# Attention scores with the high-times-low product as two 64-row matmuls, and the value halves added on GpSimd

## The chip, the cores and the metric

One NeuronCore of a Trainium2 chip runs one program. Its engines have queues of their own and meet only at semaphores: TensorE (PE in the profile, with its weight loads as PEld), VectorE (DVE), ScalarE (ACT), GpSimd (POOL) and SyncE (SP), which issues most of the transfers. The metric is the device time of the program in microseconds (us), taken as the median of several runs. One further execution is recorded by the hardware profiler, and every duration below comes from that one.

## The reference, cut to what matters

The program is a two-layer encoder on a sequence of 1024 positions with 1024 channels: layer one mixes by attention, layer two by a long convolution, and each is followed by a gated feed-forward block. The change lies in the attention, which has 16 query heads of 64 channels that share 4 key and value heads in groups of 4:

```python
q = q.reshape(Bsz, L, N_HEADS, HEAD_DIM)
k = k.reshape(Bsz, L, N_KV_HEADS, HEAD_DIM)
...
q = apply_rope(rmsnorm(q, q_gain), cos, sin)
k = apply_rope(rmsnorm(k, k_gain), cos, sin)
...
def block(q_blk):
    s = jnp.einsum('bqkgd,bskd->bkgqs', q_blk, k, preferred_element_type=jnp.float32) * scale
    p = jax.nn.softmax(s, axis=-1).astype(v.dtype)
    return jnp.einsum('bkgqs,bskd->bqkgd', p, v)
```

Everything is float32, and the output has to keep close to that. The matmuls run in a float32 format that is rounded on the way in, so the kernel splits an operand into a rounded high part and the low part that is left, and adds up products of the parts.

## The kernel before, in words

The attention is worked off in 32 blocks: 4 key heads (`g`) times 8 tiles of 128 queries (`qb`). A block `u` holds the 4 query heads that share the key head, so it has 4 scores of 128 queries by 1024 keys, and 8 steps over tiles of 128 keys (`sb`).

- **Layout of the queries and keys.** `q_t` (`load_q`, line 811) has the 64 channels of the high part in partitions 0 to 63 and those of the low part in 64 to 127. `kTh` has the high keys in both halves of the partitions, `kTl` the low keys in both halves. So a matmul of all 128 rows of `q_t` with `kTh` (line 830) is high times high plus low times high, and one with `kTl` (line 831) is high times low plus low times low. A score takes four matmuls of 512 columns: two halves of the keys, each with both products, into two banks of PSUM.
- **Softmax.** VectorE takes the row maximum from PSUM (`nmx`, line 838), ScalarE the exponential with its row sum (`p_t`, line 848).
- **The steps.** For each tile of keys TensorE transposes the four heads' probabilities into one PSUM bank (`pt_ps`, line 854), ScalarE copies the high part out (`pT_hi`, line 859), VectorE subtracts it from PSUM for the low part (`pT_lo`, recorded under the helper's line 162), and two steps later TensorE multiplies both with the values (lines 872 and 873). The values `vst` hold the high part in 64 columns and the low part in the other 64, so the accumulator `o_ps` has two halves of 64 partitions that must still be added.
- **The end of a block** (`finish`). ScalarE copies each half out of `o_ps` by two copies of 64 by 256 that put the heads in place (`o_s`, `o_l`, line 893). VectorE adds the halves (line 895). TensorE transposes the reciprocal sums, spread out on GpSimd (`rbs`, line 885), into a bank of the same three that `pt_ps` uses (`rb_ps`, line 899). VectorE multiplies (line 900), which frees that bank, and GpSimd writes the high and low part of the result (lines 902 and 903).
- **What else runs there.** GpSimd works off 24 steps of a modulation vector between the blocks (`mod_step`, lines 189 to 192: one or two passes over 128 by 1024), and issues the loads of `q_t` (line 815).

`o_ps` has one bank, `pt_ps` and `rb_ps` three, a score two at a time. The order on each engine in this stage is set by the framework's scheduler, which lays the instructions out by a simulated timeline when the program is built; after that each engine works strictly through its list. The functions that the change touches, with the lines that the profile names:

Of the kernel before, what the change touches and what calls it, by code (L numbers as in the profile page):

```python
# [7 lines left out]
F32 = mybir.dt.float32  # L8
F32R = mybir.dt.float32r
# [5 lines left out]
P = 128  # L15
# [6 lines left out]
HD = 64  # L22
# [93 lines left out]
def tile_kernel(ctx: ExitStack, tc: tile.TileContext, t: dict):  # L116
    nc = tc.nc
    mm = nc.tensor.matmul
    V = nc.vector
    ADD, SUB, MUL = ALU.add, ALU.subtract, ALU.mult  # L120
# [26 lines left out]
    qd = [tc.dram_tile([8, P, L], F32, name=f"qd{i}") for i in range(2)]  # L147
# [13 lines left out]
    def sub_lo(lo, src, hi):  # L161
        V.tensor_tensor(lo, src, hi.bitcast(F32), op=SUB)  # L162
# [140 lines left out]
    HS = (slice(0, 512), slice(512, L))  # L303
# [321 lines left out]
    with tc.tile_pool(name="x0", bufs=1) as xp:  # L625
# [7 lines left out]
        def load_ada(k):  # L633
            at = ada_tile()
            for i in (1, 0):
                nc.sync.dma_start(at[:, i], t["ada_t"][i, k])
            return at
# [33 lines left out]
        for k in range(KT):  # L671
            at = load_ada(k) if k >= ADA0 else ada0[k]
# [21 lines left out]
    kTh = [kv_pool.tile([P, L], F32R, name=f"kTh{g}") for g in range(NKV)]  # L694
    kTl = [kv_pool.tile([P, L], F32R, name=f"kTl{g}") for g in range(NKV)]
    v_pool = tc.alloc_tile_pool(name="vst", bufs=1)
    vst = [v_pool.tile([P, NKV, 2, HD], F32R, name=f"vst{j}") for j in range(NT)]
    q_pool = tc.alloc_tile_pool(name="q", bufs=4)
    at0 = tc.alloc_tile_pool(name="att0", bufs=4)
    with tc.tile_pool(name="qkv", bufs=1) as qp:  # L700
        def qtile(tag, bufs):
# [63 lines left out]
        for ch in (2, 0, 1):  # L765
# [7 lines left out]
            for j in range(NT):  # L773
                if j not in pqs:
                    pqs[j] = mt("qkv_mm", {2: "AAAABBAA", 0: "AABBAAAA", 1: "AAAABBBB"}[ch][j])
                    tj = slice(j * P, (j + 1) * P)
                    for k in range(KT):
                        wh, wl = w[k // 2]
                        cs = slice(512 * (k % 2), 512 * (k % 2) + 512)
# [26 lines left out]
    at = tc.alloc_tile_pool(name="att", bufs=1)  # L806
    s_psp = tc.alloc_tile_pool(name="att_s", bufs=1, space=PSUM)
    ps = tc.alloc_tile_pool(name="att_ps", bufs=1, space=PSUM, side="right")
    qg = {}

    def load_q(u):
        if u < NU:
            g, qb = divmod(u, NT)
            qg[u] = q_pool.tile([P, 4, P], F32R, name="q_t", tag="q_t")
            nc.gpsimd.dma_start(qg[u], qd[g // 2][4 * (g % 2):4 * (g % 2) + 4, :, qb * P:(qb + 1) * P]
                              .rearrange("h p q -> p h q"))

    NU = NKV * NT
    sums, pts, s_t, pt_t, o_t = {}, {}, {}, {}, {}

    def scores(u, i):
        if u >= NU:
            return
        g, qb = divmod(u, NT)
        if i == 0:
            load_q(u + 3)
        s_ps = s_psp.tile([P, L], F32, name="s_ps", tag="s", bufs=2)
        for hf in range(2):
            cs = slice(512 * hf, 512 * hf + 512)
            mm(s_ps[:, cs], lhsT=qg[u][:, i], rhs=kTh[g][:, cs], start=True, stop=False)  # L830
            mm(s_ps[:, cs], lhsT=qg[u][:, i], rhs=kTl[g][:, cs], start=False, stop=True)  # L831
        s_t[u, i] = s_ps

    def rowmax(u, i):
# [20 lines left out]
        pt_t[u, sb] = [tp]  # L855

    def pt_hi(u, sb):
        ph = at.tile([P, 512], F32R, name="pT_hi", tag="pT_hi", bufs=6)
        nc.scalar.copy(ph, pt_t[u, sb][0])  # L859
        pt_t[u, sb].append(ph)  # L860

    def pt_lo(u, sb):
        pl = at.tile([P, 512], F32R, name="pT_lo", tag="pT_lo", bufs=6)
        sub_lo(pl, pt_t[u, sb][0], pt_t[u, sb][1])
        pt_t[u, sb].append(pl)

# [8 lines left out]
    fin = {}  # L875

    def finish(u, step):
        if u < 0:
            return
        g, qb = divmod(u, NT)  # L880
        if step == 0:
            rinv = at.tile([P, 4], F32, name="rinv", tag="rinv", bufs=2)
            V.reciprocal(rinv, sums[u])
            rbs = at.tile([P, 4, HD], F32, name="rbs", tag="rbs", bufs=3)
            nc.gpsimd.tensor_copy(rbs, rinv.unsqueeze(2).to_broadcast([P, 4, HD]))
            fin["rbs", u] = rbs.rearrange("p (a b) d -> p a (b d)", b=2)
        elif step == 2:
            fin["ol"] = at.tile([P, 2, P], F32, name="o_l", tag="o_l", bufs=2)
            fin["os"] = at.tile([P, 2, P], F32, name="o_s", tag="o_s", bufs=2)
            for lo, nm in ((0, "os"), (HD, "ol")):  # L890
                ov = o_t[u][lo:lo + HD, :].rearrange("p (a b q) -> p b a q", b=2, q=P)
                for par in range(2):
                    nc.scalar.copy(fin[nm][par * HD:(par + 1) * HD], ov[:, par])
        elif step == 3:
            V.tensor_tensor(fin["os"], fin["os"], fin["ol"], op=ADD)
            rb = ps.tile([P, 512], F32, name="rb_ps", tag="pt", bufs=3)
            fin["rb"] = rb[:, 0:256].rearrange("p (a q) -> p a q", q=P)
            for hp in range(2):
                nc.tensor.transpose(fin["rb"][:, hp], fin["rbs", u][:, hp], ident)
            V.tensor_tensor(fin["os"], fin["os"], fin["rb"], op=MUL)  # L900
            dst = [o_[:, 2 * g:2 * g + 2, qb * P:(qb + 1) * P] for o_ in (oht, olt)]
            nc.gpsimd.tensor_copy(dst[0], fin["os"])
            nc.gpsimd.tensor_tensor(dst[1], fin["os"], dst[0].bitcast(F32), op=SUB)

    LAG, MOD0, MODD = 2, 27, 9
    for u in range(3):
        load_q(u)
    for i in range(4):
        scores(0, i)
        rowmax(0, i)  # L910
        softexp(0, i)
    steps = [(u, sb) for u in range(NU) for sb in range(NT)]
    for n in range(len(steps) + LAG):
        if n < len(steps):
            if steps[n][1] == 0:
                finish(steps[n][0], 0)
            transp(*steps[n])
            pt_hi(*steps[n])
            pt_lo(*steps[n])
        if n >= LAG:  # L920
            u, sb = steps[n - LAG]
            attend(u, sb)
            if sb == NT - 1:
                finish(u, 2)
                finish(u, 3)
        if n == 246:
            w_o0 = load_split(t["w_o"][0], w0_pool, 1)
        i, k = divmod((n - MOD0) // MODD, KT)
        if (n - MOD0) % MODD == 0 and 0 <= i < 3:
            mod_step(3 + i, ssq, k)  # L930
        if (n - MOD0) % MODD == MODD - 3 and k == KT - 1 and -1 <= i < 3:
            mod_fin(0, 3 + i, ssq, lambda: ps.tile([P, 512], F32, name="pt_ps", tag="pt", bufs=3))
        if n < len(steps):
            u, sb = steps[n]
            if sb < 4 and u + 1 < NU:
                scores(u + 1, sb)
                rowmax(u + 1, sb)
                softexp(u + 1, sb)
# [813 lines left out]
    with tc.manual_schedule(engines={mybir.EngineType.PE}):  # L1752
        w = sum(max(c - MM_CBASE, MM_CMIN) for n in range(G_END) for c in step_cost(n))
        rate = (1 + 21 * 48 + 2 * FLUSH - n_mm[0]) / w
        for n, c in conv_steps(JOBS, on_done):
            if gemm:
                owed += rate * max(c - MM_CBASE, MM_CMIN)
                need = {(1 + o, c4) for o, c4 in JOBS[:(n + 2) // 8]}
                while gemm and (owed >= 1 or n >= G_END or (n == 5 and len(ca) == 2) or need - seen):
                    g = next(gemm, None)  # L1760
# [275 lines left out]
```

## Time and profile before

| What | Value |
| --- | --- |
| Median of 3 runs (lowest, highest) | 2944.6 us (2941.42, 2945.13) |
| Profiled execution, its own time | 2945.4 us |
| Its span in the trace | 2943.4 us |
| Busy: PE / DVE / ACT / POOL | 2819.3 / 2330.6 / 1232.5 / 317.5 us |
| Attention stage in the trace | about 230 to 632 us |
| In that stretch: PE / DVE / ACT / POOL busy | 382.98 / 343.31 / 320.63 / 184.47 us |

A matmul's record runs from its start to the end of its result's way out, so neighbours overlap, and the distance between two starts says what one of them costs. "128*128" in a row is rows times columns of the array that the weights use; "128x512" is the output. "idle before" with an arrow names what ended an engine's wait.

### The profile page before, as it was taken

The numbers are of one execution on the slowest core, as the hardware profiler recorded it, in microseconds if no ns is written. First come the engines' busy times: TensorE is split into PE (matmuls) and PEld (weight loads), VectorE is DVE, ScalarE is ACT, GpSimd is POOL, SyncE is SP. The second block draws the span as 40 slices with busy tenths as digits, with TensorE's granted clock in tenths as the row PEclk, the third lists the DMA queues.
The fourth block names the chain that finished last, engine by engine and source line by source line (L and its number), as shares of the span: only waits on it lengthen the run. The fifth ranks groups of instructions, "written<-read, shape, count | busy, mean of one in ns | idle before, by whom it ended". The sixth has DMA issues, their size and how long they took to land.

```text
span 2943.4 us, 36504 instructions
## 1 busy us (share of the span) xinstructions
PE 2819.3 (96%) x13152; PEld 2301.5 (78%) x13152; DVE 2330.6 (79%) x3225; ACT 1232.5 (42%) x1996; POOL 317.5 (11%) x344
## 2 busy tenths in 40 slices
PE   5989999999999999999999999999989999999998
PEld 4777877778888887888777887887868788887887
DVE  8797989869988887877777885888978887777544
ACT  3547888843444444343332332323334433333211
POOL 0063564400000000111000000000000000000000
PEclk9999999999999999999999999999999999999999
DMA  7262222146444444755456665556664332224321
GB/s 277 91 184 63 58 74 55 52 150 210 139 164 160 164 164 172 223 174 152 159 182 194 216 211 185 184 166 200 224 208 154 122 101 86 85 79 143 122 86 58
DMA packets 220823, 433.72 MB, mean 147 GB/s; under 512 B 22146, under 2 KB 117154, under 8 KB 216164
## 3 DMA queue, kind: packets, MB, share of 16 engines
q1 hardware_dynamic: 185444, 389.44, 39.5%
q0 software_dynamic: 35200, 41.95, 5.3%
q8 instruction: 104, 1.70, 0.2%
q14 instruction: 75, 0.61, 0.1%
HBM read 304.42 MB, written 126.89 MB: 147 GB/s over the span
## 4 chain that ended last, share of the span: by engine, by line
PE 64%; DVE 9%; DMA 4%; issue 1%; ACT 1%; SPq 0%; DVEq 0%; ACTq 0%; POOLq 0%
PE w_ps L1063 26%; PE d_ps L183 14%; PE u_ps L1437 4%; PE d_ps L1296 2%; PE wo_y L183 2%; PE ab_ps L1573 2%; PE f_ps L183 2%; PE g_ps L358 2%; PE v_ps L358 1%; DVE prod L1643 1%; PE f_ps L578 1%; PE wout_y L1859 1%; PE f_ps L579 1%; PE wo_y L1036 1%; DMA rd<-fw 1%
## 5 line engine op out<-in xcount | busy, mean ns | idle before, releaser
L1155 ACT CAST w_hi<-u 128x1024 fp32r<-128x1024 f32 x120 | 125.8, 1049 | 236.0 <-PE w_ps L1063 224.7
L162 DVE TENSOR_TENSOR pT_lo<-pt_ps,pT_hi 128x512 fp32r<-128x512 f32 x256 | 167.7, 681 | 46.9 <-ACT pT_hi L859 45.2
L1063 PE MATMUL w_ps<-t_h,w_hi 128*128 128x512 f32 x480 | 190.7, 397 | 1.9 <-ACT w_hi L1155 1.9
L1261 DVE SCALAR_TENSOR_TENSOR xd<-d_ps,mod,xd 128x1024 f32<-128x1024 f32 x104 | 132.7, 1280 | 75.4 <-PE d_ps L183 75.2
L1063 PE MATMUL w_ps<-t_h,w_lo 128*128 128x512 f32 x480 | 189.9, 397 | 0.7 <-DVE w_lo L162 0.7
L162 DVE TENSOR_TENSOR w_lo<-u,w_hi 128x1024 fp32r<-128x1024 f32 x120 | 146.6, 1222 | 55.6 <-ACT w_hi L1155 55.4
L1063 PE MATMUL w_ps<-t_l,w_hi 128*128 128x512 f32 x480 | 190.2, 396 | 0.0
L859 ACT CAST pT_hi<-pt_ps 128x512 fp32r<-128x512 f32 x256 | 145.0, 588 | 69.6 <-PE pt_ps L854 63.9
L183 PE MATMUL d_ps<-s_hi,wd_lo 128*128 128x512 f32 x544 | 170.0, 391 | 0.0
L183 PE MATMUL d_ps<-s_lo,wd_hi 128*128 128x512 f32 x544 | 169.9, 391 | 0.0
L183 PE MATMUL d_ps<-s_hi,wd_hi 128*128 128x512 f32 x544 | 168.9, 390 | 0.0
L838 DVE TENSOR_REDUCE nmx<-s_ps 128x1 f32<-128x1024 f32 x128 | 155.5, 1217 | 10.8 <-PE s_ps L831 9.0
L854 PE MATMUL pt_ps<-ident,p_t 128*128 128x128 f32 x1024 | 154.4, 274 | 10.0 <-DVE pT_lo L162 9.0
L854 PEld LDWEIGHTS pt_ps<-ident,p_t 128*128 128x128 f32 x1024 | 126.6, 141 | 44.8 <-DVE pT_lo L162 7.8
L848 ACT ACTIVATE p_t<-s_ps,nmx 128x1024 f32<-128x1024 f32 x128 | 143.7, 1124 | 3.9 <-DVE nmx L838 2.7
L1437 PE MATMUL u_ps<-fh_h,w_lo 128*128 128x512 f32 x368 | 132.5, 419 | 2.4 <-DMA w_lo<-wld 2.4
L1573 PE MATMUL ab_ps<-prod,dfti 128*128 128x256 f32 x512 | 124.7, 387 | 6.8 <-DVE prod L1643 3.4
L1437 PE MATMUL u_ps<-fh_l,w_hi 128*128 128x512 f32 x368 | 127.8, 414 | 0.0
L1063 PE MATMUL w_ps<-fh_h,w_hi 128*128 128x512 f32 x320 | 124.9, 390 | 0.7 <-ACT w_hi L1155 0.7
L1063 PE MATMUL w_ps<-fh_l,w_hi 128*128 128x512 f32 x320 | 124.8, 390 | 0.0
L1063 PE MATMUL w_ps<-gh_h,w_hi 128*128 128x512 f32 x320 | 124.7, 390 | 0.0
L1063 PE MATMUL w_ps<-gh_l,w_hi 128*128 128x512 f32 x320 | 124.7, 390 | 0.0
(424 smaller groups left out, 7556.3 us busy)
## 6 DMA issues: line engine op xcount, KB each, us to landing
u<-in_w_up_dram SPq DMA_DIRECT2D x80, 512.0 KB
w_raw<-in_w_down_dram SPq DMA_DIRECT2D x44, 512.0 KB
sg<-gate SPq DMA_DIRECT2D x40, 512.0 KB
w_raw<-sg SPq DMA_DIRECT2D x40, 512.0 KB
w_raw<-in_ada_w_dram SPq DMA_DIRECT2D x32, 512.0 KB
ed<-eo SPq DMA_DIRECT2D x64, 256.0 KB
eo<-ed SPq DMA_DIRECT2D x16, 1024.0 KB
kd<-k_sb SPq DMA_DIRECT2D x64, 256.0 KB
```

The costliest lines, as they stand in the source:

```text
L162: V.tensor_tensor(lo, src, hi.bitcast(F32), op=SUB)
L183: mm(out[:, cs], lhsT=a, rhs=b[:, cs], start=start and i == 0, stop=stop and i == 2)
L358: mm(pp[:, HS[hf]], lhsT=(wh, wh, wl)[i][:, ks], rhs=hd[hf][i % 2][k], start=k == 0 and i == 0, stop=k == n - 1 and i == 2)
L838: V.tensor_reduce(nmx, s_t[u, i], op=ALU.max, axis=AX.X, negate=True)
L848: nc.scalar.activation(p_t, s_ps, AF.Exp, bias=nmx, accum_out=sums[u][:, i:i + 1])
L854: nc.tensor.transpose(tp[:, i * P:(i + 1) * P], pts[u, i][:, sb * P:(sb + 1) * P], ident)
L859: nc.scalar.copy(ph, pt_t[u, sb][0])
L1063: mm(out, lhsT=(w[0], w[0], w[1])[i][:, k * P:(k + 1) * P], rhs=b[i % 2][k], start=k == 0 and i == 0, stop=k == 3 and i == 2)
L1155: nc.scalar.copy(w[0], src)
L1261: ins = V.scalar_tensor_tensor(x[dt_], yp, gate[dt_], x[dt_], op0=MUL, op1=ADD)
L1437: mm(yp[:, HS[hf]], lhsT=(wh, wh, wl)[i][:, k * P:(k + 1) * P], rhs=hd[hf][i % 2][k], start=k == 0 and i == 0, stop=k == KT - 1 and i == 2)
L1573: mm(ap[:, i], lhsT=dfti[:, m, :], rhs=v, start=n == 0, stop=n == len(ops) - 1)
```

## The change

A query tile gets a second copy, in which the high part lies in partitions 64 to 127 (a second load of 64 partitions). Both products with the high keys are as before. The product with the low keys becomes high times low alone: the first half of the keys is multiplied in rows 0 to 63 of the array and the second half in rows 64 to 127, by two matmuls of 64 rows into two banks. The product of low with low is left out. The two halves of `o_ps` leave PSUM by two copies of 64 by 512, and GpSimd adds them, by two adds of 64 by 256 that put the heads in place; VectorE's add is gone. To make room, `q_t` has 3 buffers (each twice as large) for 4, the split probabilities 5 for 6, `rbs` 2 for 3, and a query tile is asked for two blocks ahead instead of three.

```diff
-    q_pool = tc.alloc_tile_pool(name="q", bufs=4)
+    q_pool = tc.alloc_tile_pool(name="q", bufs=3)
...
-            qg[u] = q_pool.tile([P, 4, P], F32R, name="q_t", tag="q_t")
-            nc.gpsimd.dma_start(qg[u], qd[g // 2][4 * (g % 2):4 * (g % 2) + 4, :, qb * P:(qb + 1) * P]
-                              .rearrange("h p q -> p h q"))
+            qg[u] = q_pool.tile([P, 2, 4, P], F32R, name="q_t", tag="q_t")
+            src = qd[g // 2][4 * (g % 2):4 * (g % 2) + 4, :, qb * P:(qb + 1) * P].rearrange("h p q -> p h q")
+            nc.gpsimd.dma_start(qg[u][:, 0], src)
+            nc.gpsimd.dma_start(qg[u][HD:P, 1], src[0:HD])
...
         if i == 0:
-            load_q(u + 3)
+            load_q(u + 2)
         s_ps = s_psp.tile([P, L], F32, name="s_ps", tag="s", bufs=2)
         for hf in range(2):
-            cs = slice(512 * hf, 512 * hf + 512)
-            mm(s_ps[:, cs], lhsT=qg[u][:, i], rhs=kTh[g][:, cs], start=True, stop=False)
-            mm(s_ps[:, cs], lhsT=qg[u][:, i], rhs=kTl[g][:, cs], start=False, stop=True)
+            mm(s_ps[:, HS[hf]], lhsT=qg[u][:, 0, i], rhs=kTh[g][:, HS[hf]], start=True, stop=False)
+        for hf in range(2):
+            rows = slice(HD * hf, HD * hf + HD)
+            mm(s_ps[:, HS[hf]], lhsT=qg[u][rows, hf, i], rhs=kTl[g][rows, HS[hf]], start=False, stop=True)
...
-        ph = at.tile([P, 512], F32R, name="pT_hi", tag="pT_hi", bufs=6)
+        ph = at.tile([P, 512], F32R, name="pT_hi", tag="pT_hi", bufs=5)
...
-        pl = at.tile([P, 512], F32R, name="pT_lo", tag="pT_lo", bufs=6)
+        pl = at.tile([P, 512], F32R, name="pT_lo", tag="pT_lo", bufs=5)
...
-            rbs = at.tile([P, 4, HD], F32, name="rbs", tag="rbs", bufs=3)
+            rbs = at.tile([P, 4, HD], F32, name="rbs", tag="rbs", bufs=2)
...
         elif step == 2:
-            fin["ol"] = at.tile([P, 2, P], F32, name="o_l", tag="o_l", bufs=2)
             fin["os"] = at.tile([P, 2, P], F32, name="o_s", tag="o_s", bufs=2)
-            for lo, nm in ((0, "os"), (HD, "ol")):
-                ov = o_t[u][lo:lo + HD, :].rearrange("p (a b q) -> p b a q", b=2, q=P)
-                for par in range(2):
-                    nc.scalar.copy(fin[nm][par * HD:(par + 1) * HD], ov[:, par])
+            parts = []
+            for i in range(2):
+                o_i = at.tile([HD, 512], F32, name=f"o_{i}", tag=f"o_{i}", bufs=1)
+                nc.scalar.copy(o_i, o_t[u][i * HD:(i + 1) * HD])
+                parts.append(o_i.rearrange("p (a b q) -> p b a q", b=2, q=P))
+            for par in range(2):
+                nc.gpsimd.tensor_tensor(fin["os"][par * HD:(par + 1) * HD], parts[0][:, par], parts[1][:, par], op=ADD)
         elif step == 3:
-            V.tensor_tensor(fin["os"], fin["os"], fin["ol"], op=ADD)
...
-    for u in range(3):
+    for u in range(2):
         load_q(u)
```

The scheduler lays the whole stage out anew. The first place is TensorE around one score in the middle of the stage, before:

```order
L873 MATMUL o_ps<-pT_lo,vst_465 128x512
L899 MATMUL rb_ps<-ident,rbs 128x128 x2
L830 MATMUL s_ps<-kTh_447,q_t 128x512
L831 MATMUL s_ps<-kTl_451,q_t 128x512
L830 MATMUL s_ps<-kTh_447,q_t 128x512
L831 MATMUL s_ps<-kTl_451,q_t 128x512
L854 MATMUL pt_ps<-ident,p_t 128x128 x6
```

and in the changed kernel (830 is still the product with the high keys, 833 the two 64-row ones, 856 the transposes, 902 those of the sums):

```order
L875 MATMUL o_ps<-pT_lo,vst_465 128x512
L830 MATMUL s_ps<-kTh_448,q_t 128x512 x2
L833 MATMUL s_ps<-kTl_452,q_t 128x512 x2
L902 MATMUL rb_ps<-ident,rbs 128x128 x2
L856 MATMUL pt_ps<-ident,p_t 128x128 x4
```

High and low products alternated; now the two of one kind stand together. Of the 128 pairs at line 833, 127 are adjacent like this one, between matmuls that use all 128 rows.

The second place is VectorE at the end of a block. Before, the add and the multiplication (895, 900) come ahead of the low part of the first `pt_ps` that TensorE fills after `rb_ps`, which is `pt_ps_2876`:

```order
L162 TENSOR_TENSOR pT_lo_2850<-pt_ps_2843,pT_hi_2848 128x512
L838 TENSOR_REDUCE nmx_2913<-s_ps_2908 128x1
L895 TENSOR_TENSOR o_s_2855<-o_s_2855,o_l_2854 128x256
L900 TENSOR_TENSOR o_s_2855<-o_s_2855,rb_ps_2861 128x256
L162 TENSOR_TENSOR pT_lo_2883<-pt_ps_2876,pT_hi_2881 128x512
```

In the changed kernel the first `pt_ps` after `rb_ps_2869` is `pt_ps_2884`, and the multiplication (903) that frees `rb_ps_2869` stands here:

```order
L162 TENSOR_TENSOR pT_lo_2891<-pt_ps_2884,pT_hi_2889 128x512
L162 TENSOR_TENSOR pT_lo_2912<-pt_ps_2905,pT_hi_2910 128x512
L840 TENSOR_REDUCE nmx_3030<-s_ps_3025 128x1
L162 TENSOR_TENSOR pT_lo_2932<-pt_ps_2925,pT_hi_2930 128x512
L162 TENSOR_TENSOR pT_lo_2943<-pt_ps_2936,pT_hi_2941 128x512
L162 TENSOR_TENSOR pT_lo_2954<-pt_ps_2947,pT_hi_2952 128x512
L840 TENSOR_REDUCE nmx_3051<-s_ps_3046 128x1
L162 TENSOR_TENSOR pT_lo_2969<-pt_ps_2962,pT_hi_2967 128x512
L162 TENSOR_TENSOR pT_lo_2984<-pt_ps_2977,pT_hi_2982 128x512
L840 TENSOR_REDUCE nmx_3071<-s_ps_3066 128x1
L162 TENSOR_TENSOR pT_lo_3008<-pt_ps_3001,pT_hi_3006 128x512
L903 TENSOR_TENSOR o_s_2862<-o_s_2862,rb_ps_2869 128x256
```

So the bank of `rb_ps` stays taken while eight later tiles pass through the other two. Counted over the 32 blocks, before it is none or one such tile; in the changed order it is six to nine in 15 blocks and none to four in the other 17.

The third place is GpSimd, where the adds (897) stand in one list with the modulation steps (191 and 192), the loads of `q_t` (816, 817) and the rest of the block's end (887, 905, 906):

```order
L816 DMA q_t_2988<-qd0_82 128x4x128
L817 DMA q_t_2988<-qd0_82 64x4x128
L905 CAST oh_1877<-o_s_2712 128x2x128
L887 COPY rbs_2975<-rinv_2973 128x256
L192 TENSOR_TENSOR ssq_74<-ssq_74,w_raw_3284 128x1024
L897 TENSOR_TENSOR o_s_2862<-o_0_2863,o_1_2865 64x256 x2
L191 TENSOR_SCALAR w_raw_3471<-w_raw_3471,csil_69 128x1024
```

The adds that VectorE's row 903 waits for stand behind a pass over 128 by 1024 and a load.

## The prediction

> **What bounds the kernel now.** I read the page's first and fourth part, then the stretch of the attention by engine, then its groups, then single matmuls in the timeline.
>
> ```profile
> PE 2819.3 (96%) x13152; PEld 2301.5 (78%) x13152; DVE 2330.6 (79%) x3225; ACT 1232.5 (42%) x1996; POOL 317.5 (11%) x344
> PE 64%; DVE 9%; DMA 4%; issue 1%; ACT 1%; SPq 0%; DVEq 0%; ACTq 0%; POOLq 0%
> 230.00:632.00 402.00, 382.98 (x2180) 307.94 (x2180) 343.31 (x480) 320.63 (x630) 184.47 (x165) 0.99 0.21 55
> ```
>
> TensorE carries the chain over the whole program. The third row is the attention: 402 us long, busy times in the order PE, weight loads, DVE, ACT, POOL, then a granted clock of 0.99. Three engines are at 80% or more there, so "PE 95%" does not settle it. A PE record holds its way out too, so I count starts instead.
>
> ```profile
> 501.67 0.40 PE L830 MATMUL s_ps<-kTh,q_t 128*128 128x512 f32 x1
> 502.83 0.39 PE L831 MATMUL s_ps<-kTl,q_t 128*128 128x512 f32 x1
> 499.85 0.60 PE L854 MATMUL pt_ps<-ident,p_t 128*128 128x128 f32 x4
> L854 PE MATMUL pt_ps<-ident,p_t 128*128 128x128 f32 x1024 | 154.4, 274 | 10.0 <-DVE pT_lo L162 9.0 <-ACT q_out L754 1.0
> ```
>
> The first two rows are the first and the last of six score matmuls in one run: (502.83 - 501.67) / 5 = 0.23 us each. Four transposes take 0.60 us with one record of 0.274 us at the end, so (0.60 - 0.274) / 3 = 0.11 us each.
>
> In the stretch stand 1024 transposes and 64 of the sums (1088 x 0.11 = 120 us), 512 matmuls with the values, 476 of the scores and 40 of the next stage (1028 x 0.23 = 236 us): 356 of 402 us. For VectorE and ScalarE the busy time is true occupation, 343 and 321 us. So TensorE leads, by little, and 46 us of the stretch are its gaps. What VectorE and ScalarE cause of them in whole stalls is small:
>
> ```profile
> PE pt_ps L854 <- DVE pT_lo L162: 9.0, 8, 2.0
> PE o_ps L872 <- ACT pT_hi L859: 3.0, 2, 1.6
> PE o_ps L873 <- DVE pT_lo L162: 1.3, 4, 0.6
> PE o_ps L872 <- ACT o_l L893: 0.8, 2, 0.4
> ```
>
> Together 14.1 us (the columns are total, times, longest). The rest are gaps shorter than a record's way out.
>
> **The low product.** On paper a score goes from four slots to three: two whole matmuls, and two of 64 rows side by side. Before, the stage uses the whole array alone ("128*128"). What it costs to leave that and come back is seen elsewhere in the trace, where a part of the array is used between whole matmuls:
>
> ```profile
> 642.32 0.39 PE L183 MATMUL wo_y<-oh,w_lo 128*128 128x512 f32 x1
> 642.63 1.07 PE L423 MATMUL mlp_ps<-fh_h,fh_h 33*64 33x512 f32 x2
> 643.63 0.50 PE L183 MATMUL wo_y<-ol,w_hi 128*128 128x512 f32 x1
> 643.97 0.39 PE L183 MATMUL wo_y<-oh,w_lo 128*128 128x512 f32 x1
> 643.63 0.19 PEld L183 LDWEIGHTS wo_y<-ol,w_hi 128*128 128x128 f32 x1 [0.81 <-issue]
> 643.74 0.19 PEld L183 LDWEIGHTS wo_y<-oh,w_lo 128*128 128x128 f32 x1
> 1246.17 0.39 PE L183 MATMUL d_ps<-s_hi,wd_hi 128*128 128x512 f32 x1
> 1246.49 1.02 PE L534 MATMUL f_ps<-macc,ones 128*1 128x256 f32 x4
> 1247.79 0.40 PE L183 MATMUL d_ps<-s_lo,wd_hi 128*128 128x512 f32 x1
> 1531.49 0.59 PE L584 MATMUL f_ps<-u,dftf 128*1 128x256 f32 x2
> L584 PE MATMUL f_ps<-u,dftf x16: 377/377/378, 1531.5 to 1806.5; 128*1 128x256 f32 x16
> ```
>
> The reader should see that the matmul after such a change starts 0.31 to 0.32 us after the last one (642.32 to 642.63, 1246.17 to 1246.49), not 0.23, and its weights load only then, while inside a run they load ahead. The way back has the same: load at 643.63, the second matmul only 0.34 us later. I take out the streaming. The last two rows give it for this unrounded kind: (0.59 - 0.377) = 0.21 us for 256 columns, so 0.42 for 512. The first excursion lasts 643.97 - 642.32 = 1.65 us; minus two whole slots (0.46) and two times 0.42 leaves 0.35. The second lasts 1.62 us; minus 0.46 and four times 0.21 leaves 0.32. I take **0.33 us for out and back**, twice a load in the open and twice the end of the matmul before.
>
> A changed score pays that, plus the pair. Lower end: both halves stream together, one slot of 0.23; 0.33 + 0.23 - 0.46 = +0.10 us. Upper end: one after the other; 0.33 + 0.46 - 0.46 = +0.33 us. Below both lies the case that cutting rows alone costs no way out and back: 0.23 - 0.46 = -0.23 us. No row shows rows cut without columns (33*64 cuts both, 128*1 the columns), so it stays open. I take side by side, with the second half's weights loaded behind the first's: rows 643.63 and 643.74 show loads 0.11 us apart where nothing hides them, so +0.21 us. Times 128 scores: bounds -29, +13, +42, **taken +27 us**.
>
> The Trainium skill, "TensorEngine Tiling (Array Packing)", section Key Properties, says that changing the tiling mode drains TensorE, which speaks against this change; the trace agrees as far as it goes, with the 0.31 us above. "TensorE: Matmul & The Clock Gate", Part 3, has tiles of different rows start about 4 ns apart, their loads overlapped; by that rule the term would be the lower end, and that is a rival below.
>
> **What is taken off VectorE and ScalarE.**
>
> ```profile
> L895 DVE TENSOR_TENSOR o_s<-o_s,o_l 128x256 f32<-128x256 f32 x32 | 28.7, 896 | 3.1 <-ACT o_l L893 3.1
> L895 DVE TENSOR_TENSOR o_s<-o_s,o_l x32: 415/417/3220, 247.8 to 630.9; 128x256 f32<-128x256 f32 x32
> L893 ACT COPY o_l<-o_ps 64x256 f32<-64x256 f32 x64 | 23.6, 369 | 1.2
> L859 ACT CAST pT_hi<-pt_ps 128x512 fp32r<-128x512 f32 x256 | 145.0, 588 | 69.6 <-PE pt_ps L854 63.9 <-DMA qd<-q_out 2.3 <-PE o_ps L872 0.4
> L162 DVE TENSOR_TENSOR pT_lo<-pt_ps,pT_hi 128x512 fp32r<-128x512 f32 x256 | 167.7, 681 | 46.9 <-ACT pT_hi L859 45.2
> ```
>
> VectorE loses 28.7 us of adds (median 0.417 us, at worst 3.22). ScalarE trades four copies of 0.369 for two of 512 columns, 0.588 by the nearest row: (1.476 - 1.176) x 32 = 9.6 us less, and `o_ps` is free 0.3 us sooner. Both are off the leading engine; their worth is at most the stalls above, between 0 and 14.1 us. Since what is freed (38 us) is more than that, I take **-14 us**.
>
> **The bank held by the sums.** The scheduler now puts the multiplication that frees `rb_ps` six to nine tiles late in 15 of 32 blocks, so transposes run on two banks there. A bank's round is four transposes, the copy and the subtraction, 0.60 + 0.588 + 0.681 = 1.87 us. A step takes 402 / 256 = 1.57 us, so two banks allow 3.14, fine unless an exponential and a row maximum both stand in front:
>
> ```profile
> L848 ACT ACTIVATE p_t<-s_ps,nmx 128x1024 f32<-128x1024 f32 x121 | 136.0, 1124 | 3.1 <-DVE nmx L838 1.9 <-PE pt_ps L854 0.6
> L838 DVE TENSOR_REDUCE nmx<-s_ps 128x1 f32<-128x1024 f32 x120 | 146.0, 1217 | 7.1 <-PE s_ps L831 5.2
> ```
>
> Then it is 1.87 + 1.12 + 1.22 = 4.21, over by 1.07 us, at most once for each of 15 x 4 scores: bounds 0 and 64 us. The nearest row is today's stall on `pT_lo`, 9.0 us; I take as much again, **+9 us**.
>
> **GpSimd's part, the loads, the rest.**
>
> ```profile
> L903 POOL TENSOR_TENSOR ol<-o_s,oh 128x256 fp32r<-128x256 f32 x31 | 22.9, 738 | 1.2
> L815 POOL DMA_DIRECT2D q_t<-qd x26 | 21.3, 819 | 77.3 <-PE s_ps L831 62.9 <-PE o_ps L872 11.0 <-PE pt_ps L854 3.4
> L191 POOL TENSOR_SCALAR w_raw<-w_raw,csil 128x1024 f32<-128x1024 f32 x20 | 57.0, 2848 | 0.1
> L192 POOL TENSOR_TENSOR ssq<-ssq,w_raw 128x1024 f32<-128x1024 f32 x21 | 50.1, 2388 | 0.2
> q_t<-qd POOLq DMA_DIRECT2D x32, 256.0 KB, 3.4
> ```
>
> 64 adds of 256 columns at 0.738 are 47 us, 32 more load issues at 0.819 are 26 us: POOL goes from 184 to 257 of 402 us. It is hidden as long as VectorE's row 903 finds the add done. Where it doesn't, every `pT_lo` behind it waits, and with them the transposes; the order leaves room of half a block, so I take 0, and the other end is a rival. A query tile lands 3.4 us after issue and is asked for two blocks (25 us) ahead: 0. Fewer buffers for split probabilities: two steps lag needs three of five: 0. At the stage's end the last block goes through two adds (1.48) instead of one (0.42), less 0.3 of copies: **+1 us**.
>
> Sum: +27 - 14 + 9 + 1 = +23 us on the profiled execution's 2945.4 us, which is within 1 us of the median 2944.6: **2968 us**.
>
> **The rivals.**
> 1. *Cutting rows alone costs no way out and back* (faster). -29 - 14 + 9 + 1 = -33, but TensorE falls to 327 us, beside 314 and 311 on VectorE and ScalarE, so the others' gaps come forward and a third is lost: -22, **2923 us**. For it: both excursions shown also cut columns. Against: 33*64 and 128*1 cost the same, as if any change of shape did.
> 2. *Both halves start together.* +13 - 14 + 9 + 1 = +9, **2954 us**. For it: they share no rows and no bank. Against: no row shows loads overlapping in the open.
> 3. *The halves run one after the other.* +42 - 14 + 9 + 1 = +38, **2983 us**. Nothing in this trace shows two matmuls at once.
> 4. *GpSimd's add comes late.* 21 modulation passes of 2.85 + 2.39 us stand in its list; if an add sits behind half of one each time, VectorE stands 21 x 2.6 = 55 us, of which its 59 us of free time in the stretch cover about half: +27 on the sum, **2995 us**. It decides as soon as the add lands after the eighth `pT_lo`.
>
> **How the numbers follow.** Forecast 0.42, rivals 0.21, 0.15, 0.11, 0.11. Half of rival 1's own spread (2915 to 2931) falls below 2924, rival 4 reaches above 2998; a range of 2924 to 2998 leaves out about 0.10 and 0.06. The forecast's own range is 2955 to 2982. A change under 0.2% (6 us) can't be told from none here. Faster: rival 1 and a little of 2, 0.24; within 0.2%: part of 2, 0.07; slower: the rest, 0.69.
>
> **What would show it.** At line 833: the first 64-row matmul 0.31 us after a whole one, the second 0.11 later, the next whole one's load in the open; 0.23 and loads ahead would be rival 1, a start under 0.05 apart rival 2, 0.21 or more rival 3. The stretch should be some 425 us long. TensorE's waits for `pT_lo` should be near 18 us, and VectorE's row 903 should hardly wait for POOL; a wait of tens of us is rival 4. The forecast is wrong if the stretch is under 400 us.

## The result, and the profile after

| | Before | After |
| --- | --- | --- |
| Median (lowest, highest), 4 runs each | 2943.35 us (2941.42, 2945.13) | 2969.84 us (2967.77, 2970.86) |
| Ratio, with its 95% interval | | 1.0089 (1.0074 to 1.0105) |
| Span of the profiled execution | 2943.4 us | 2968.1 us |
| Last write of `oh`, which ends the attention | 631.9 us | 657.6 us |

The changed kernel is 26.5 us, or 0.9%, slower. The stage starts at the same place and ends 25.7 us later, and the span is 24.7 us longer: the whole loss lies in the attention stage. The page's first part and the first row of its fourth:

```profile
PE 2837.9 (96%) x13152; PEld 2262.9 (76%) x13152; DVE 2306.5 (78%) x3193; ACT 1230.7 (41%) x1934; POOL 385.3 (13%) x440
PE 63%; DVE 8%; DMA 4%; issue 1%; ACT 1%; SPq 0%; POOL 0%; DVEq 0%; ACTq 0%; POOLq 0%
```

VectorE has lost 24 us and GpSimd gained 68, and TensorE has gained 19 with the same number of instructions; its share of the chain is nearly what it was (63% for 64%). The busy times of the stage, over its new length (PE, weight loads, DVE, ACT, POOL, then the granted clock):

```profile
230.00:658.00 428.00, 404.46 (x2174) 275.14 (x2173) 320.82 (x446) 315.57 (x563) 248.72 (x257) 0.99 0.26 60
```

VectorE is busy 321 us in 428, where it was 343 in 402. So it works less and the stage is longer; the clock is what it was. The timeline around one score shows what the two 64-row matmuls cost. Columns: start, duration, engine, line, operation, shape, count, and in brackets the idle time of the engine before it.

```profile
485.23 0.62 PE L830 MATMUL s_ps<-kTh,q_t 128*128 128x512 f32 x2
...
485.78 0.19 PEld L833 LDWEIGHTS s_ps<-kTl,q_t 64*128 64x128 f32 x2 [0.36 <-issue]
485.78 0.51 PE L833 MATMUL s_ps<-kTl,q_t 64*128 64x512 f32 x2
...
486.21 0.19 PEld L874 LDWEIGHTS o_ps<-pT_hi,vst 128*128 128x128 f32 x1 [0.25 <-issue]
486.22 0.50 PE L874 MATMUL o_ps<-pT_hi,vst 128*128 128x512 f32 x1
...
486.56 0.38 PE L856 MATMUL pt_ps<-ident,p_t 128*128 128x128 f32 x2
```

The two halves stand in one row with one start and 0.51 us for two records of 0.50 each, so they run at once. But the way out and back is there: the second whole matmul starts at 485.46, the pair 0.32 later, its weights loaded in the open; the next whole load comes at 486.21, 0.43 after the pair's start, and the matmul after that only 0.34 later. From 485.23 to 486.56 are 1.33 us, less three whole slots of 0.23: **0.64 us for the low product, where two whole matmuls took 0.46**. That is 0.18 us times 128 scores, 22 to 23 us of TensorE's time.

The waits of the stage (total us, times, longest):

```profile
PEld s_ps L833 <- issue: 43.8, 119, 0.7
DVE nmx L840 <- PE s_ps L833: 39.7, 32, 2.1
PEld pt_ps L856 <- DVE pT_lo L162: 22.0, 53, 0.9
PE pt_ps L856 <- DVE pT_lo L162: 11.9, 28, 0.6
PE o_ps L875 <- DVE pT_lo L162: 1.0, 3, 0.4
DVE o_s L903 <- POOL o_s L897: 4.1, 2, 3.4
PE wo_y L183 <- DVE o_s L903: 3.4, 1, 3.4
```

The first row is the way out, once at nearly every pair: the weights of the next kind are not loaded ahead. The second is new in size. The third and fourth are the transposes, which wait until VectorE's subtraction (`pT_lo`) has freed a bank: the third is the wait of their weight loads, the fourth that of the matmuls themselves, and both can hold the same idle time. In the kernel before, the matmuls' row had 9.0 us in eight waits, and the second and third rows were:

```profile
DVE nmx L838 <- PE s_ps L831: 6.7, 5, 2.2
PEld pt_ps L854 <- DVE pT_lo L162: 7.8, 5, 2.4
```

So TensorE now waits for a free bank in many short waits, where it had a few longer ones.

The last rows show that GpSimd's adds came in time but for two, though each costs as much as an operation on 128 partitions. Their groups in the stage (busy us, mean ns, then idle before):

```profile
L897 POOL TENSOR_TENSOR o_s<-o,o 64x256 f32<-64x256 f32 x64 | 47.7, 746 | 50.2 <-ACT o L894 47.6
L906 POOL TENSOR_TENSOR ol<-o_s,oh 128x256 fp32r<-128x256 f32 x32 | 24.3, 761 | 1.8
L894 ACT COPY o<-o_ps 64x512 f32<-64x512 f32 x64 | 37.2, 581 | 6.0 <-PE o_ps L875 5.6
L816 POOL DMA_DIRECT2D q_t<-qd x27 | 22.2, 821 | 70.8 <-PE s_ps L833 69.1 <-issue 1.7
L817 POOL DMA_DIRECT2D q_t<-qd x27 | 17.2, 638 | 0.0
```

### The profile page after: what moved, and what is told of

Its sections match the earlier page's. It is cut to its first block, busy times and chain, and to the rows that moved or that the text cites. A ratio compares the mean times of both kernels' runs of the same rounds, so it can differ in the third digit from the quotient of the medians.

```text
span 2968.1 us, 36587 instructions
## 1 busy us (share of the span) xinstructions
PE 2837.9 (96%) x13152; PEld 2262.9 (76%) x13152; DVE 2306.5 (78%) x3193; ACT 1230.7 (41%) x1934; POOL 385.3 (13%) x440
## 4 chain that ended last, share of the span: by engine, by line
PE 63%; DVE 8%; DMA 4%; issue 1%; ACT 1%; SPq 0%; POOL 0%; DVEq 0%; ACTq 0%; POOLq 0%
PE w_ps L1066 26%; PE d_ps L183 14%; PE u_ps L1440 5%; PE d_ps L1299 2%; PE wo_y L183 2%; PE ab_ps L1576 2%; PE f_ps L183 2%; PE g_ps L358 1%; PE f_ps L578 1%; PE v_ps L358 1%; PE f_ps L579 1%; DVE prod L1646 1%; PE wout_y L1862 1%; DMA rd<-fw 1%; PE z_ps L1555 1%
## 5 line engine op out<-in xcount | busy, mean ns | idle before, releaser
L856 PE MATMUL pt_ps<-ident,p_t 128*128 128x128 f32 x1024 | 156.9, 277 | 15.0 <-DVE pT_lo L162 11.9
L856 PEld LDWEIGHTS pt_ps<-ident,p_t 128*128 128x128 f32 x1024 | 120.5, 141 | 59.3 <-DVE pT_lo L162 22.0
```

Source lines behind the costliest of these rows:

```text
L856: nc.tensor.transpose(tp[:, i * P:(i + 1) * P], pts[u, i][:, sb * P:(sb + 1) * P], ident)
```

## The experiments

Where one kernel is compared with another, each is taken as its distance from the kernel before on the same chip; those distances are in the table at the end of this section.

**The cut alone.** The kernel before with the score part of the change: second copy of the queries, 64-row pair, three buffers of `q_t`, five of the split probabilities. The end of a block stays as it was, and the order on the engines nearly so (the bank of `rb_ps` is held by the same 11 tiles, in the same blocks).

```diff
+            nc.gpsimd.dma_start(qg[u][HD:P, 1], src[0:HD])
...
-            mm(s_ps[:, cs], lhsT=qg[u][:, i], rhs=kTl[g][:, cs], start=False, stop=True)
+        for hf in range(2):
+            rows = slice(HD * hf, HD * hf + HD)
+            mm(s_ps[:, HS[hf]], lhsT=qg[u][rows, hf, i], rhs=kTl[g][rows, HS[hf]], start=False, stop=True)
```

> Kernel before with the score part of the change alone (second query copy, two 64-row matmuls for the low product, 3 query buffers, 5 buffers for the split probabilities); the end of a block stays as before. Theory, the way out and back sets it: the changed kernel's trace shows (0.325 + 0.43 + 0.11 - 0.23) = 0.635 us for the low product of a score against 0.46, so +0.175 x 128 = +22 us on 2943.4, 2966 us. Rival, the stage is slower for the GpSimd add and the bank held by the sums, and the cut is hidden in TensorE's gaps: 2943 to 2948 us.

Measured: 2958.78 us, ratio 1.005 (1.0037 to 1.0063), +14.2 us. The cut costs time by itself, as the forecast said, but 14 of the 22 us of TensorE's time that it takes: part of it falls into gaps that were there. An estimate from the distances between starts fits that: between 300 and 500 us, what is left beside the slots and the way out and back is 15 us before and 9 here.

**The block's end alone.** The kernel before with the two copies of 64 by 512, the two adds on GpSimd and two buffers of `rbs`; scores as before.

```diff
+                nc.scalar.copy(o_i, o_t[u][i * HD:(i + 1) * HD])
...
+                nc.gpsimd.tensor_tensor(fin["os"][par * HD:(par + 1) * HD], parts[0][:, par], parts[1][:, par], op=ADD)
...
-            V.tensor_tensor(fin["os"], fin["os"], fin["ol"], op=ADD)
```

> Kernel before with the end of a block alone as in the change (two copies, GpSimd adds, 2 buffers for the spread sums). In this order the bank of the sums is never held past one tile, so the +9 us of the held bank drop out. Theory by the prediction's sum: -14 + 1 = -13 us, 2930 us. Rival, the work taken off VectorE and ScalarE was never in front of TensorE: 2943 to 2945 us. Rival, VectorE waits for GpSimd's add behind the modulation passes: 2950 us or more.

Measured: 2957.56 us, ratio 1.0041 (1.0027 to 1.0054), +13.0 us. What the expectation says of the held bank is wrong: in the order as it is laid out, `rb_ps` is held over 86 later tiles in all, up to five in a block. Taking 28.7 us of adds off VectorE made the kernel slower. Its waits:

```profile
DVE nmx L838 <- PE s_ps L831: 34.2, 23, 2.4
PE pt_ps L854 <- DVE pT_lo L162: 8.4, 13, 2.0
PE o_ps L873 <- DVE pT_lo L162: 7.8, 16, 0.8
```

The row maxima wait for scores five times as long as before, though nothing in the scores was touched. With the cut alone this wait is 3.9 us. The two parts together (14.2 + 13.0) make 27.2 us, and the whole change measures 26.5: they add up.

**The change with whole low products.** As the changed kernel, but the low keys are multiplied in all 128 rows again, so low times low is back in.

```diff
-            rows = slice(HD * hf, HD * hf + HD)
-            mm(s_ps[:, HS[hf]], lhsT=qg[u][rows, hf, i], rhs=kTl[g][rows, HS[hf]], start=False, stop=True)
+            mm(s_ps[:, HS[hf]], lhsT=qg[u][:, 0, i], rhs=kTl[g][:, HS[hf]], start=False, stop=True)
```

> Changed kernel with the low product as two matmuls of all 128 rows from the first query copy, as before; everything else, the order of the stage and the held bank included, as in the change. It computes low times low again. Theory, the cut costs 0.175 us a score and TensorE's time comes through one to one: 2969.8 - 22 = 2947 us. Rival, the stage is held by something else and the cut is hidden: 2965 to 2970 us.

Measured: 2962.24 us, ratio 1.006 (1.0047 to 1.0073), +17.7 us. The larger part of the loss is still there without the cut. The cut on top of this is worth 26.5 - 17.7 = 9 us, with about 6 of uncertainty either way. That lies between the theory and the rival, nearer the rival. TensorE's wait for a free bank stands here too: 21.1 us of the matmuls, 22.9 of the weight loads.

**Both halves in the same rows.** As the changed kernel, but both halves are multiplied in rows 0 to 63.

```diff
-            mm(s_ps[:, HS[hf]], lhsT=qg[u][rows, hf, i], rhs=kTl[g][rows, HS[hf]], start=False, stop=True)
+            mm(s_ps[:, HS[hf]], lhsT=qg[u][0:HD, 0, i], rhs=kTl[g][0:HD, HS[hf]], start=False, stop=True)
```

> Changed kernel with both halves of the low product in rows 0 to 63, so that they can't run side by side; the way out and back is the same. Theory, the pair does run at once in the change (starts 3 to 4 ns apart) and TensorE leads: one more slot of 0.23 us x 128 = +29 us, 2999 us. Rival, the two of a pair only look alike in the records and already take turns: 2970 us.

Measured: 2992.5 us, ratio 1.0164 (1.015 to 1.0178), 21.5 us over the changed kernel (48.0 - 26.5), some 6 either way. Its timeline at one score:

```profile
482.43 0.63 PE L830 MATMUL s_ps<-kTh,q_t 128*128 128x512 f32 x2
...
482.99 0.73 PE L832 MATMUL s_ps<-kTl,q_t 64*128 64x512 f32 x2
...
483.65 0.74 PE L830 MATMUL s_ps<-kTh,q_t 128*128 128x512 f32 x2
```

Now the pair's two records last 0.73 us together, where it was 0.51, and the next whole matmul starts 0.66 us after the pair, where it was 0.44: one whole slot more, and 128 x 0.22 = 28 us of TensorE's time. So in the change the halves do run side by side, and rival 3 is out.

**Two banks for the transposes.** The kernel before with two buffers of `pt_ps` and `rb_ps` for three.

```diff
-        tp = ps.tile([P, 512], F32, name="pt_ps", tag="pt", bufs=3)
+        tp = ps.tile([P, 512], F32, name="pt_ps", tag="pt", bufs=2)
```

> Kernel before with two banks for transposes and sums instead of three; nothing else. The price of a bank that is missing all the time. With the end of a block alone changed, the order held the bank over 86 tiles in 32 blocks (at most 5 in one; the expectation of that run had said none, which was wrong), a third of 256. Theory, the held bank is what made that run 13 us slower: three times as much or more here, 2943 + 39 and up, 2982 to 3020 us. Rival, the scheduler lays the order out around two banks and the stage hardly needs the third: under 2955 us.

Measured: 3020.3 us, ratio 1.0264 (1.0244 to 1.0284), +76.9 us.

```profile
DVE nmx L838 <- PE s_ps L831: 65.5, 34, 2.3
PEld pt_ps L854 <- DVE pT_lo L162: 57.4, 132, 0.8
PE pt_ps L854 <- DVE pT_lo L162: 32.9, 85, 0.9
```

A bank that is missing all the time is dear, so the third one is needed; by proportion, 86 tiles of 256 would be worth 26 us, which no run measures. It is not a clean price: the order is laid out anew here too, and the wait of the row maxima has grown as well.

**VectorE's add left out.** The kernel before without line 895, so the low half of the values does not reach the output; the copies stay.

```diff
-            V.tensor_tensor(fin["os"], fin["os"], fin["ol"], op=ADD)
```

> Kernel before without VectorE's add of the two halves; the low half of the values is left out of the result, the copies out of PSUM stay. No work goes to GpSimd. The order holds the bank over no tile. Theory by the prediction's relief term, 28.7 us less on VectorE let TensorE's waits go: 2930 to 2937 us. Rival, VectorE was never in front and its relief is worth nothing: 2942 to 2945 us. Rival, any relief makes the scheduler lay out an order that is worse on the chip: 2950 us or more.

Measured: 2920.42 us, ratio 0.9921 (0.9903 to 0.9938), -23.0 us. Two stretches in the middle of the stage, of the kernel before and then of this one:

```profile
300.00:400.00 100.00, 97.06 (x554) 78.44 (x553) 89.12 (x124) 82.41 (x164) 52.67 (x46) 0.98 0.23 58
400.00:500.00 100.00, 97.87 (x569) 79.02 (x568) 92.42 (x128) 83.66 (x166) 52.62 (x46) 1.00 0.24 62
```

```profile
300.00:400.00 100.00, 100.00 (x589) 82.16 (x588) 87.86 (x124) 87.28 (x176) 57.49 (x50) 1.00 0.25 64
400.00:500.00 100.00, 100.00 (x592) 82.15 (x590) 88.79 (x124) 86.93 (x175) 56.54 (x50) 1.00 0.24 64
```

TensorE's records leave no idle time, and 4 to 6% more of its instructions fit into the same stretch (589 for 554, 592 for 569). The distances between starts also show gaps that are shorter than a record's way out; by an estimate from them, some 15 us of gaps in these 200 become some 5. So VectorE does hold TensorE back before, by more than the waits show, and a relief of 28.7 us there can bring 23, together with the order that comes with it (no bank is held here). The change doesn't get this. This is the run that moved the question: not what the relief is worth, but what takes it away again.

The adds themselves, in the kernel before, show one way in which VectorE was in front. Twenty of the 32 take 0.415 to 0.426 us. In the other twelve an instruction of GpSimd (lines 191, 192 or 903) runs beside the add, and it takes 0.88 to 3.22 us: 15.4 of the 28.7 us are this stretching. Three of the twelve look like this one:

```profile
272.31 3.21 DVE L895 TENSOR_TENSOR o_s<-o_s,o_l 128x256 f32<-128x256 f32 x1
272.84 2.39 POOL L192 TENSOR_TENSOR ssq<-ssq,w_raw 128x1024 f32<-128x1024 f32 x1
275.44 0.68 DVE L162 TENSOR_TENSOR pT_lo<-pt_ps,pT_hi 128x512 fp32r<-128x512 f32 x1
...
276.18 0.55 PE L854 MATMUL pt_ps<-ident,p_t 128*128 128x128 f32 x3 [1.97 <-DVE pT_lo L162]
```

The add ends 0.3 us after GpSimd's pass, the `pT_lo` behind it is late, and TensorE stands 2 us. The three make 6 of the 9.0 us that the transposes wait for `pT_lo` before. No run takes GpSimd's passes away, so that they stretch the add rests on the twelve and the twenty.

**The block's end, sums later.** The block's end alone as above, with the transposes of the sums, the multiplication and what follows it (`finish` step 3) moved six steps later, into the next block. The bank is then held over 3 tiles where it was 86.

```diff
-                finish(u, 3)
+            if sb == 6:
+                finish(u - 1, 3)
...
+    finish(NU - 1, 3)
```

> The end of a block alone as in the change (two copies, GpSimd adds), with the transposes of the sums and the multiplication moved six steps later in the program, when the add is done; the order holds the bank over 3 tiles in all instead of 86. Theory, the held bank cost the 13 us: 2930 to 2944 us. Rival, the cost comes from elsewhere (GpSimd's list, the order of the scores): 2953 to 2960 us.

Measured: 2941.0 us, ratio 0.9994 (0.9985 to 1.0004), 15 us less than the block's end alone. But no gain over before:

```profile
POOL rbs L885 <- PE rb_ps L900: 98.4, 20, 15.8
DVE nmx L838 <- PE s_ps L831: 36.9, 24, 2.6
PE pt_ps L854 <- DVE pT_lo L162: 11.0, 16, 0.9
```

With the bank free again the row maxima still wait as long. And GpSimd now stands 98 us for one of the two `rbs`, so the 15 us can't be put down to the hold alone.

**The change, sums later.** The same move in the changed kernel; 17 tiles held where it was 136.

```diff
-                finish(u, 3)
+            if sb == 6:
+                finish(u - 1, 3)
```

> The changed kernel with the same move; the order holds the bank over 17 tiles in all instead of 136. Theory, what is left is the cut's price, 2943 + 14 = 2957, less some relief: 2950 to 2958 us. Rival, the held bank is not what costs: 2966 to 2970 us.

Measured: 2960.46 us, ratio 1.0057 (1.0041 to 1.0073), 9.5 us less than the change, with some 6 either way, and between the theory and the rival. The waits are like those of the run above (87.1 us for `rbs`, 38.3 us of the row maxima). TensorE's wait for a free bank has fallen to about that of the kernel before (9.0 and 7.8 us): 9.3 us of the matmuls for 11.9 in the change, 5.1 of the weight loads for 22.0.

**The cut where TensorE has no gaps.** The score part of the change, in the kernel without VectorE's add; the order is that of the kernel without the add.

```diff
+            mm(s_ps[:, HS[hf]], lhsT=qg[u][rows, hf, i], rhs=kTl[g][rows, HS[hf]], start=False, stop=True)
...
-            V.tensor_tensor(fin["os"], fin["os"], fin["ol"], op=ADD)
```

> The score part of the change on top of the kernel without VectorE's add (the low half of the values is left out of the result); the order on TensorE and VectorE is the one of that kernel, whose TensorE had no idle time by its records for 200 us on end. Theory, where TensorE has no gaps the cut costs its full 0.175 us x 128 = 22 us: 2920 + 22 = 2942 us. Rival, the cut's price is 14 us or less as on the kernel before, for another reason than gaps: 2928 to 2935 us.

Measured: 2938.34 us, ratio 0.9984 (0.9973 to 0.9995), -5.8 us, so 17 us over the kernel without the add, with 6 of uncertainty. TensorE is busy 100.00 of 100 us in both stretches here too. That fits a way out and back that comes through nearly whole where nothing hides it, and less with gaps; but 17 and the 14.2 above are too close to be told apart.

**One whole add on GpSimd, sums four steps later.** The kernel before, its four copies kept; the add of 128 by 256 moves from VectorE to GpSimd.

```diff
+            nc.gpsimd.tensor_tensor(fin["os"], fin["os"], fin["ol"], op=ADD)
...
-            V.tensor_tensor(fin["os"], fin["os"], fin["ol"], op=ADD)
...
-                finish(u, 3)
+            if sb == 4:
+                finish(u - 1, 3)
```

> Kernel before with its four copies of 64 by 256, the add as one of 128 by 256 on GpSimd instead of VectorE, and the sums' transposes and the multiplication four steps later in the program; the order holds the bank over one tile in all. Theory, relief without a held bank: 2920 to 2932 us. Rival, the order in which two scores follow each other on TensorE costs what the relief brings: 2938 to 2946 us.

Measured: 2950.88 us, ratio 1.0026 (1.0015 to 1.0037), +6.7 us, slower than both forecasts. The bank is held over a single tile, and still the row maxima wait 50.9 us.

**The same, two steps later.**

```diff
-            if sb == 4:
+            if sb == 2:
```

> The same with two steps instead of four; the bank is held over 20 tiles in all, and in many blocks the scores stand apart as before. Theory of the held bank: 2 to 4 us more than with four steps. Rival of the order: as fast or faster than with four steps.

Measured: 2939.41 us, ratio 0.9989 (0.9979 to 0.9999), -4.7 us, and 11 us faster than with four steps, as the rival said. It is the fastest of the kernels that leave nothing out, though its interval ends just short of no change. The bank is held over 20 tiles here, and the row maxima wait 21.7 us.

**The move alone.** The kernel before, VectorE's add kept, with only the four-step move.

```diff
-                finish(u, 3)
+            if sb == 4:
+                finish(u - 1, 3)
```

> Kernel before with the four-step move alone, VectorE's add kept. The price of the order that the move brings, in which two scores follow each other on TensorE. Theory, the held bank and VectorE's load are what counts: 2940 to 2946 us. Rival, such an order costs by itself: 2952 us or more.

Measured: 2959.38 us, ratio 1.0055 (1.0041 to 1.007), +15.2 us. No instruction is added or removed and the bank is held over no tile, yet this costs as much as either part of the change. Its waits:

```profile
DVE nmx L838 <- PE s_ps L831: 56.8, 26, 2.5
PE o_ps L873 <- DVE pT_lo L162: 21.8, 28, 1.8
PE pt_ps L854 <- DVE pT_lo L162: 3.6, 4, 2.6
```

All kernels beside each other. "Held" is the number of later tiles over which the bank of the sums is kept, and "doubles" how often two scores follow each other on TensorE with nothing between them but the transposes of the sums, both counted in the order that each kernel was laid out in; the last column is the wait of VectorE's row maxima for a score.

| Kernel | us against before | Held | Doubles | Row maxima wait, us |
| --- | --- | --- | --- | --- |
| before | 0 | 11 | 9 | 6.7 |
| cut alone | +14.2 | 11 | 10 | 3.9 |
| add left out | -23.0 | 0 | 5 | 10.3 |
| cut, add left out | -5.8 | 0 | 6 | 8.5 |
| one add on GpSimd, 2 later | -4.7 | 20 | 17 | 21.7 |
| block's end, 6 later | -2.4 | 3 | 29 | 36.9 |
| one add on GpSimd, 4 later | +6.7 | 1 | 29 | 50.9 |
| block's end alone | +13.0 | 86 | 23 | 34.2 |
| move alone | +15.2 | 0 | 32 | 56.8 |
| change, 6 later | +17.0 | 17 | 30 | 38.3 |
| change, whole low products | +17.7 | 136 | 26 | 38.9 |
| the change | +26.5 | 136 | 26 | 39.7 |
| the change, same rows | +48.0 | 136 | 26 | 52.6 |
| two banks | +76.9 | - | 34 | 65.5 |

Wherever the add goes to GpSimd or the sums come later, the scheduler puts scores two at a time more often (17 to 32 places, where it was 9), and the row maxima then wait for them. The move alone shows that the order can cost 15 us with no bank held and no work added. That it is the doubling of scores in this order, and not another of its differences, is not shown: no kernel here changes it alone or has the add on GpSimd in the old order, and one row speaks against it, the block's end with sums six steps later, which has 29 doubles and a wait of 36.9 us and is no slower than before.

Nor does the move alone price what the order does in the change, because TensorE loses its time at another place. The next table is an estimate from the traces: the distances between TensorE's starts in the stage, each less the usual one of the same sequence of instructions, added up by what TensorE was about to start.

| Kernel | Lost ahead of transposes, us | Lost ahead of the product with `pT_lo`, us |
| --- | --- | --- |
| before | 14 | 5 |
| add left out | 7 | 2 |
| move alone | 12 | 28 |
| change, 6 later | 19 | 3 |
| change, whole low products | 39 | 3 |
| the change | 29 | 2 |
| two banks | 77 | 2 |

In the move alone `pT_lo` comes late as an operand, while no bank is held. In the change it comes late as the read that frees a bank, as with two banks, and less so once the hold is undone. So beside the cut, the traces of the change point to the held bank. What keeps the 23 us of relief away once the hold is undone stays open: the change with sums later is still 17 us slower than before, and the cut alone makes 14 of that.

## Why the prediction was right in its total and wrong in its parts

- **The total and the place.** 2968 us was predicted and 2969.84 measured; the stretch is 428 us for the 425 named, and the loss lies there. But two errors cancel in it, so that the total is this close by luck: the cut alone is +14 us and not +27, and the rest of the change is +13 and not -4.
- **The way out and back.** Shown as reasoned. The pair starts 0.32 us after the last whole matmul, for the 0.31 read from excursions that cut columns too, and the next whole load lies in the open. Rows cut without columns pay the same, so rival 1 falls.
- **The halves' start.** Here the step failed that put the second half 0.11 us behind the first. By the start times of the trace 127 of the 128 pairs start 3 to 4 ns apart. The Trainium skill, "TensorE: Matmul & The Clock Gate", Part 3, has tiles of different rows start about 4 ns apart, and the trace agrees. But rival 2, which had this start, made a score +0.10 us, and the timeline shows +0.18: the pair does not give TensorE back after one slot, the next weights come only 0.43 us after its start. The term was +0.21 us a score and measured 0.18; 22 us of TensorE's time, not 27. It is near because two errors meet here too: no 0.11 for a later start, but 0.4 for out and back where 0.33 was taken.
- **From TensorE's time to the program's.** The step that added these 27 us whole to the span failed as well. 22 us of TensorE's time gave 14.2 (3.8 either way) in the kernel before, where it has gaps, and 17 (6 either way) where its records show none.
- **VectorE's relief, -14.** The step "their worth is at most the stalls above" is wrong: leaving the add out brings 23 us. The stalls that a view of waits lists left out the gaps that are shorter than a record's way out, and most of these closed too. Nor did the prediction ask why an add with a median of 0.417 us took 3.22 at worst, though three such adds made 6 of the 14.1 us that it listed. In the change, nothing of the 23 is left.
- **The held bank, +9.** Undoing the hold brings 9 us back in the change and 15 in the block's end alone, with the order altered in the same move. The size is plausible and not cleanly measured. The place was right, but the sign was too narrow: the matmuls' wait for `pT_lo` is 11.9 us and not near 18, while that of their weight loads went from 7.8 to 22.0, and both fall when the hold is undone. That 9 fits is luck: of the 9.0 us it was taken from, 6 came from the three long adds and not from a bank.
- **What was missing: the order.** The prediction looked at the new order for the bank alone. It never asked where the scores stand. The wait of the row maxima for a score went from 6.7 to 39.7 us, and the move alone shows that an order can cost 15 us. What the order costs in the change is not measured.
- **GpSimd.** Its busy time is 249 us for the 257 worked out, the loads cost 0.82 and 0.64 us for two times 0.819, and VectorE's multiplication waited for it 4.1 us in two places. Rival 4 did not come about, and the 0 for this part was right. The end of the stage waits 3.4 us for the last block where it was 2.8, near the +1 said.

## What to carry to other kernels

A pair of row halves that stands alone between whole matmuls can cost more than the slots it saves: price the way out and back, here 0.4 us each time, before counting slots. Bound what a relief can bring by leaving the work out, not by the waits that a profile lists, since gaps shorter than a record are in none of them; and where an instruction's longest time is far from its median, look at what ran beside it. Where a scheduler lays out the order, a change at one engine moves all of them: compare where the work of the leading engines stands, and run such a move with the work unchanged.

## What the runs showed of the hardware

- Two matmuls of 64 rows and 512 columns in different rows of the array run at once (0.51 us for both records, 0.73 in the same rows). The way out costs the same for rows cut alone as for cut columns: 0.32 us from the last whole matmul's start here, 0.31 to 0.32 in the excursions that cut columns, one of them with rows and one without. The Trainium skill, "TensorEngine Tiling (Array Packing)", section Key Properties, says that changing the mode drains TensorE; the trace agrees as far as it goes, with 43.8 us that the weight loads wait at 119 pairs.
- An add of 64 by 256 on GpSimd takes 0.746 us in the change, and one of 128 by 256 takes 0.737 us in the run with one whole add and four steps: half the partitions save nothing, so two of them in place of one doubled the time.
- VectorE's add of two tiles in SBUF, 128 by 256, takes 0.42 us, and 0.88 to 3.22 us in each of the twelve blocks in which a GpSimd instruction ran beside it. The multiplication of the same size, which reads one operand from PSUM, takes 0.39 to 0.42 us in all 32, the five with a GpSimd instruction beside it among them.
- A copy of 64 by 512 from PSUM on ScalarE takes 0.581 us, against two of 64 by 256 at 0.369.
